# Squared key norms of the delta-rule branch from the diagonals of the key gram products

## Chip, cores and metric

The kernel runs on one core of one Trainium2 chip. The metric is the device time of one execution in microseconds, of which the median over several runs is given. Times inside an execution come from one profiled execution.

## What is computed

One layer of a diffusion backbone over 512 latent tokens with 256 context tokens, width 1024: modulated RMSNorm, one input projection that feeds two token mixers, their merge, then an expert-retrieval network and a final norm. The change lies in the first mixer, a bidirectional gated delta rule with 8 heads of 128 and chunks of 64 tokens. Of its reference this matters:

```python
def _l2norm(x):
    return x * lax.rsqrt(jnp.sum(x * x, axis=-1, keepdims=True) + EPS)
...
    k = _l2norm(_heads(k, A_HEADS))
...
    kb = k * beta[..., None]
    m = jnp.where(strict, jnp.einsum('bhnid,bhnjd->bhnij', kb, k) * decay, 0.0)
    a = m + jnp.eye(CHUNK, dtype=m.dtype)
...
    sol = lax.linalg.triangular_solve(a, rhs, left_side=True, lower=True, unit_diagonal=True)
```

So each head needs the norms of its 768 keys, and for each of its 12 chunks the 64x64 products of all keys with one another.

## The kernel before

The program has a prologue (norms, modulation, gates), the first branch (delta rule), the second branch (a gated linear scan), a tail of projections, the merge, and the expert network. The input projection is cut into 88 groups of 128 columns. Each group is done by `proj` as three matmuls per block of 128 rows (`mm3`, lines 103 to 105: the weights are split into a high and a low part), into the tiles `pcl` (512 latent columns) and `pcx` (256 context columns). The groups that the second branch and the merge need are called fills: `spill` projects them and sends them to DRAM, and they may be done at any time.

The first branch works head by head. `prepare(h)` makes what does not depend on the running state: the decays `E_`, the key norms, the chunk products `gl_`, the factors `br` (lines 572 to 574) and `brS` (576, 578) out of norms and gates, the inverse of each chunk's triangular matrix, then query, value and gate. `scan(h)` runs the 12 steps of the state recurrence in both directions. A step is a matmul of state and keys (L728, from its second step on), a DVE operation that makes `tmp` (L733), a matmul with the inverse (L735), a DVE operation that makes `vd` (L738), two matmuls for the new state (L744) and two DVE operations on the state (L752 copies into `sc_`, or L754).

Keys lie with their 128 channels on the partitions, tokens along the free axis (`kt`). Before, `norms(kt, 6)` squared them on ScalarE (L530) and summed over the partitions with matmuls against a column of ones (L532, one per block of 128 tokens, into the PSUM tile `pn`); `rsqrt` adds the epsilon on DVE (L195) and takes the power on GpSimd (L199). Then `gl_` is made by 12 matmuls of a chunk's keys with themselves (L570), each into one half of the partitions. The decays are multiplied by `br` on GpSimd (L582) and by `gl_` on DVE (L583). Of the product the 16x16 diagonal blocks are masked (`C_`, L587), summed into `D16` (L589) and sent through DRAM into `prob` (L595), where they are inverted (L599 to L616). The same function `norms` serves the queries.

The generators are interleaved: `weave` advances `scan(h)`, `prepare(h + 1)`, the rows of the modulation (`bacc`, `bw`) and the fills in fixed proportions, a piece from one `yield` to the next. On what they emit a scheduler then sets the order on each engine, with buffers and dependencies; each engine runs its own order strictly, but for weight loads. Also in the DVE order stand the low parts of the weights (`wlo`, L99), one per projection group.

Of the kernel before, what the change touches and what calls it, by code (L numbers as in the profile page):

```python
# [9 lines left out]
F32 = mybir.dt.float32  # L10
# [6 lines left out]
OP = mybir.AluOpType  # L17
AX = mybir.AxisListType.X
# [45 lines left out]
def program(nc, tc, A, out, dbg=None):  # L64
    V, S, G, T, Y = nc.vector, nc.scalar, nc.gpsimd, nc.tensor, nc.sync
# [18 lines left out]
    def bm(ap, n):  # L84

        return ap[:, None, :].to_broadcast([ap.shape[0], n, ap.shape[1]])
# [25 lines left out]
    def hct(shape, name, dt=F32):  # L112
        return hp.tile(shape, dt, name=name)
# [7 lines left out]
    ones1 = cst([128, 1], "ones1")  # L121
    m_st = [hct([128, 64], f"m_st{d}") for d in range(2)]
    m_in = [hct([128, 64], f"m_in{d}") for d in range(2)]
    m_in2 = hct([128, 2, 64], "m_in2")
    lvl2 = [hct([128, 2, 64], f"lvl2_{s}") for s in range(2)]
    dm4 = hct([128, 4, 16], "dm4")
# [13 lines left out]
    j64 = tmp_.tile([128, 64], I32, name="j64")  # L140
# [6 lines left out]
        G.iota(pl[s], pattern=[[0, 64]], base=0, channel_multiplier=1)  # L147
    V.tensor_scalar(m_st[0], j64, 0.0, None, op0=OP.is_lt)
    V.tensor_scalar(m_st[1], j64, 0.0, None, op0=OP.is_gt)
    V.tensor_scalar(m_in[0], j64, 0.0, None, op0=OP.is_ge)  # L150
    V.tensor_scalar(m_in[1], j64, 0.0, None, op0=OP.is_le)
    xr = tmp_.tile([128, 64], I32, name="xr")
# [41 lines left out]
    def rsqrt(dst, src, scale=1.0, eps=EPS):  # L194
        V.tensor_scalar(dst, src, scale, eps, op0=OP.mult, op1=OP.add)  # L195
        n = 1
        for x in dst.shape[1:]:
            n *= x
        G.tensor_tensor(dst, dst, mhalf[:dst.shape[0], :n], op=OP.pow)  # L199
# [15 lines left out]
    def bank(shape, name):  # L215
        return ps.tile(shape, F32, name=name, tag="a", bufs=3)
# [41 lines left out]
    with tc.tile_pool(name="p0", bufs=1) as p0:  # L258
# [41 lines left out]
        for k in range(KD):  # L300
            for z, bs in ((0, (0, 1, 2, 3)), (1, (4, 5))):
                pt = bank([128, NL], "pt")
                n = 128 * len(bs)
                for i, b in enumerate(bs):
# [6 lines left out]
                                                       op=OP.subtract)  # L311
# [96 lines left out]
    def blk(c, ctx):  # L408
        return (4 if ctx else 0) + c // 2, slice(64 * (c % 2), 64 * (c % 2) + 64), c % 2
# [63 lines left out]
    with tc.tile_pool(name="pA", bufs=1) as pA:  # L473
# [17 lines left out]
        def col(b):  # L491
            return b * 128 + (1 if b >= 4 else 0)

        def head(t, h):

            return t.rearrange("p b (d h) -> p d b h", d=2)[:, :, :, h]
# [30 lines left out]
        def norms(src, n):  # L527
            pn = bank([128, 8], "pn")
            sq = pA.tile([128, WG], F32, name="sq", tag="cv", bufs=CVB)
            S.activation(sq[:, :src.shape[1]], src, AF.Square)  # L530
            for b in range(n):
                T.matmul(pn[:, b:b + 1], sq[:, col(b):col(b) + 128], ones1, start=True, stop=True)  # L532
            r = pA.tile([128, n], F32, name=f"rn{n}", bufs=2)
            rsqrt(r, pn[:, :n])
            return r

        def ksl(kt, c, ctx):
            o = (NL + 1 if ctx else 0) + 64 * c
            return kt[:, o:o + 64]
# [9 lines left out]
        def prepare(h):  # L549
            if h == 0:  # L550
                yield from keys(0)
            kt = KT[h]
# [8 lines left out]
            S.activation(E_, E_, AF.Abs)  # L561
            S.activation(E_, E_, AF.Exp, scale=-1.0)
            yield
            rnk = bm(norms(kt, 6), 2)
            yield

            gl_ = bank([128, 6, 64], "gl_")
            for c in range(12):
                b, s, _ = blk(c % 8, c >= 8)
                T.matmul(gl_[s, b], ksl(kt, c % 8, c >= 8), ksl(kt, c % 8, c >= 8), start=True, stop=True)  # L570
            br = pA.tile([128, 3, 2, 6], F32, name="br", bufs=2)
            V.tensor_tensor(br[:, 0], head(beta, h), rnk, op=OP.mult)
            V.scalar_tensor_tensor(br[:, 1], br[:, 0], -1.0, rnk, op0=OP.mult, op1=OP.mult)
# [202 lines left out]
        rows_ = ada_rows()  # L776
        fill = chain(*fill)
        weave((prepare(0), 44), (fill, F0, True))
        for h in range(NH):
            weave((scan(h), WS), (prepare(h + 1) if h + 1 < NH else iter(()), 44), (rows_, 9, True),  # L780
                  (fill, FH if h < NH - 1 else FL, True))
# [678 lines left out]
```

## Time and profile before

| | |
|---|---|
| median of 3 runs | 2686.17 us (2684.44 to 2699.28) |
| profiled execution | 2690.35 us |
| its span | 2688.5 us |
| TensorE (PE) busy | 2499.1 us, 93% |
| TensorE weight loads (PEld) | 2097.6 us, 78% |
| VectorE (DVE) | 1867.9 us, 69% |
| ScalarE (ACT) | 1101.5 us, 41% |
| GpSimd (POOL) | 1142.4 us, 42% |

Busy time is the time in which an engine executes instructions of the kind named; PE and PEld overlap. An fp32 matmul shows as two rows. The idle time in brackets behind a row of a timeline is that of its engine just before it, with the instruction that ended it. The chain of waits is followed back from an engine's last instruction to what released it. The clock in the windows is TensorE's granted clock as a share of 2.4 GHz; its other level is 1.2 GHz.

### The profile page before, as it was taken

To read this page: it belongs to the slowest core of one execution; us is meant where nothing else is said; L and a number is where in the kernel's file an instruction comes from. 1 tells how busy PE (TensorE), PEld (TensorE's weight loads), DVE (VectorE), ACT (ScalarE), POOL (GpSimd) and SP (SyncE) were. 2 spreads that over 40 slices of the span, in tenths; PEclk is the share of its full clock that TensorE was granted. 3 is DMA by queue.
4 is the path that set the end of the run, shared out by engine and by line. 5 is a ranking of instruction groups with operands and counts; after the bars stand their busy time and mean duration, and the time that the engine had idled before them with its cause. 6 is when DMAs were issued, how large, how long until landed. Compare 5 with 4: busy or idle time off the path is not lost.

```text
span 2688.5 us, 40933 instructions
## 1 busy us (share of the span) xinstructions
PE 2499.1 (93%) x15664; PEld 2097.6 (78%) x15664; DVE 1867.9 (69%) x3260; ACT 1101.5 (41%) x1657; POOL 1142.4 (42%) x670
## 2 busy tenths in 40 slices
PE   6999999999999888999999878999999999999997
PEld 3777777777777767777778878898899989988886
DVE  6654565464464478834569998796887778778888
ACT  3533343343442466624322345455433333333333
POOL 2322233133240244300010555564577767777784
PEclk9999999899999989999999988999999999999999
DMA  5322233333241323336442477797898888899994
GB/s 213 102 80 77 79 105 95 84 94 99 82 115 60 122 96 106 110 114 200 161 144 90 144 247 269 265 321 249 291 362 315 314 307 312 308 327 331 328 327 157
DMA packets 247829, 511.08 MB, mean 190 GB/s; under 512 B 58784, under 2 KB 129856, under 8 KB 243536
## 3 DMA queue, kind: packets, MB, share of 16 engines
q1 hardware_dynamic: 190032, 318.64, 36.6%
q0 software_dynamic: 36864, 134.23, 13.9%
q10 hardware_dynamic: 20736, 55.58, 5.5%
q8 instruction: 123, 2.02, 0.3%
q14 instruction: 74, 0.61, 0.1%
HBM read 441.94 MB, written 66.44 MB: 189 GB/s over the span
## 4 chain that ended last, share of the span: by engine, by line
PE 63%; DVE 19%; DMA 5%; issue 5%; POOL 5%; ACT 3%; SPq 1%; DVEq 0%; POOLq 0%; ACTq 0%
PE oacc L104 6%; PE oacc L105 6%; PE oacc L103 6%; PE pcl L103 4%; PE pcl L105 4%; PE pcl L104 4%; PE pS L105 4%; PE pS L103 4%; PE pS L104 4%; DVE oh L1264 2%; DVE oh L1260 2%; DVE gscr L1126 2%; PE quad L744 2%; DVE wlo L99 1%; PE pq L105 1%
## 5 line engine op out<-in xcount | busy, mean ns | idle before, releaser
L99 DVE TENSOR_TENSOR wlo<-wraw,whi 128x1024 fp32r<-128x1024 f32 x328 | 511.6, 1560 | 199.2 <-ACT whi L98 189.7
L98 ACT CAST whi<-wraw 128x1024 fp32r<-128x1024 f32 x384 | 402.4, 1049 | 563.2 <-PE pS L104 158.4
L103 PE MATMUL pS<-tTh,whi 128*128 128x384 f32 x1024 | 351.2, 343 | 16.1 <-ACT afx L1024 15.2
L105 PE MATMUL pS<-tTh,wlo 128*128 128x384 f32 x1024 | 350.2, 342 | 11.9 <-POOL wlo L99 8.0
L104 PE MATMUL pS<-tTl,whi 128*128 128x384 f32 x1024 | 348.5, 340 | 0.0
L103 PE MATMUL oacc<-whi,ah 128*128 128x512 f32 x768 | 299.5, 390 | 5.1 <-ACT ah L1331 5.1
L105 PE MATMUL oacc<-whi,al 128*128 128x512 f32 x768 | 300.4, 391 | 0.9 <-DVE al L1332 0.9
L104 PE MATMUL oacc<-wlo,ah 128*128 128x512 f32 x768 | 300.2, 391 | 0.0
L103 PE MATMUL pcl<-hTh,whi 128*128 128x512 f32 x704 | 298.8, 424 | 0.0
L1327 POOL TENSOR_TENSOR ag<-af,gread 128x384 f32<-128x384 f32 x128 | 229.7, 1795 | 142.4 <-DVE al L1332 124.7
L104 PE MATMUL pcl<-hTl,whi 128*128 128x512 f32 x704 | 288.4, 410 | 0.0
L105 PE MATMUL pcl<-hTh,wlo 128*128 128x512 f32 x704 | 288.0, 409 | 0.0
L1123 POOL DMA_INDIRECT gr<-in_u_rows,eidx x128 | 188.3, 1471 | 133.8 <-DVE gscr L1126 98.3
L1123 POOL DMA_INDIRECT gr<-in_v_rows,eidx x128 | 210.5, 1644 | 41.2 <-DVE gacc L1130 20.4
L99 POOL TENSOR_TENSOR wlo<-wraw,whi 128x1024 fp32r<-128x1024 f32 x56 | 145.7, 2605 | 178.7 <-PE psc L1160 98.3
L103 PEld LDWEIGHTS pS<-tTh,whi 128*128 128x128 f32 x1024 | 196.6, 192 | 19.0 <-ACT afx L1024 15.8
L105 PEld LDWEIGHTS pS<-tTh,wlo 128*128 128x128 f32 x1024 | 196.3, 192 | 14.3 <-POOL wlo L99 9.5
L104 PEld LDWEIGHTS pS<-tTl,whi 128*128 128x128 f32 x1024 | 196.4, 192 | 2.0
L1331 ACT CAST ah<-ag 128x384 fp32r<-128x384 f32 x128 | 65.7, 513 | 300.3 <-PE oacc L104 289.8
L103 PEld LDWEIGHTS oacc<-whi,ah 128*128 128x128 f32 x768 | 144.6, 188 | 34.2 <-ACT ah L1331 5.6
L105 PEld LDWEIGHTS oacc<-whi,al 128*128 128x128 f32 x768 | 144.4, 188 | 31.7 <-DVE al L1332 1.6
L1126 DVE SCALAR_TENSOR_TENSOR gscr<-gr,ttk 128x1024 bf16<-128x1024 f32 x128 | 168.3, 1315 | 1.0
(1199 smaller groups left out, 5115.1 us busy)
## 6 DMA issues: line engine op xcount, KB each, us to landing
wraw<-in_u_t SPq DMA_DIRECT2D x128, 512.0 KB
wraw<-in_v_rows SPq DMA_DIRECT2D x128, 512.0 KB
wraw<-in_w_c SPq DMA_DIRECT2D x88, 512.0 KB
GD<-gst ACTq DMA_DIRECT2D x24, 1024.0 KB
gread<-GD SPq DMA_DIRECT2D x128, 192.0 KB
bw<-in_w_ada SPq DMA_DIRECT2D x64, 256.0 KB
afD<-afx ACTq DMA_DIRECT2D x64, 192.0 KB
af<-afD SPq DMA_DIRECT2D x64, 192.0 KB
```

Source lines behind the costliest of these rows:

```text
L98: S.copy(hi, raw)
L99: (eng or V).tensor_tensor(lo, raw, hi.bitcast(F32), op=OP.subtract)
L103: T.matmul(o, Lh, Rh, start=first, stop=False)
L104: T.matmul(o, Lh, Rl, start=False, stop=False)
L105: T.matmul(o, Ll, Rh, start=False, stop=last)
L744: T.matmul(po_[d], ktm[s, b], vd[s], start=True, stop=True)
L1123: G.indirect_dma_start(out=r, out_offset=None, in_=A["u_rows" if i < NSEL else "v_rows"], in_offset=IndirectOffsetOnAxis(ap=eidx[:, n:n + ...
L1126: x = V.scalar_tensor_tensor(scr, r, 1.0, ttk, op0=OP.mult, op1=OP.mult, accum_out=gs[:, n:n + 1])
L1260: V.tensor_tensor(oh1, io2[:, None].to_broadcast([128, 8, 128, 2]), over(sel[:, (tg * GT + t8) // 8].rearrange("p z t -> p (z t)")), op=OP ...
L1264: held[0] = V.tensor_tensor(oh2[:, 4 * z:4 * z + 4], oh1[:, 4:8], over(ghl[:, z, ts]), op=OP.mult)
L1327: G.tensor_tensor(ag.rearrange("p (g t) -> p g t", t=GT), af.rearrange("p (g t) -> p g t", t=GT), gr[:, :, e % EG, :], op=OP.mult)
L1331: S.copy(ah, ag)
```

## The change

The norms of the keys are no longer computed by `norms`. A mask `d64`, one where token and partition agree within a chunk, is made once. After the products `gl_` DVE multiplies them with the mask (`gd`) and sums over the 64 columns (`rnk`), which leaves each key's squared norm on the partition of its token; `rsqrt` follows as before. With `norms` one of the two `yield`s around it goes. The queries' norms are as they were.

```diff
--- before.py
+++ after.py
@@ -121,6 +121,7 @@
     ones1 = cst([128, 1], "ones1")
     m_st = [hct([128, 64], f"m_st{d}") for d in range(2)]
     m_in = [hct([128, 64], f"m_in{d}") for d in range(2)]
+    d64 = hct([128, 64], "d64")
     m_in2 = hct([128, 2, 64], "m_in2")
     lvl2 = [hct([128, 2, 64], f"lvl2_{s}") for s in range(2)]
     dm4 = hct([128, 4, 16], "dm4")
@@ -147,6 +148,7 @@
         G.iota(pl[s], pattern=[[0, 64]], base=0, channel_multiplier=1)
     V.tensor_scalar(m_st[0], j64, 0.0, None, op0=OP.is_lt)
     V.tensor_scalar(m_st[1], j64, 0.0, None, op0=OP.is_gt)
+    V.tensor_scalar(d64, j64, 0.0, None, op0=OP.is_equal)
     V.tensor_scalar(m_in[0], j64, 0.0, None, op0=OP.is_ge)
     V.tensor_scalar(m_in[1], j64, 0.0, None, op0=OP.is_le)
     xr = tmp_.tile([128, 64], I32, name="xr")
@@ -561,13 +563,18 @@
             S.activation(E_, E_, AF.Abs)
             S.activation(E_, E_, AF.Exp, scale=-1.0)
             yield
-            rnk = bm(norms(kt, 6), 2)
-            yield
 
             gl_ = bank([128, 6, 64], "gl_")
             for c in range(12):
                 b, s, _ = blk(c % 8, c >= 8)
                 T.matmul(gl_[s, b], ksl(kt, c % 8, c >= 8), ksl(kt, c % 8, c >= 8), start=True, stop=True)
+
+            gd = pA.tile([128, 6, 64], F32, name="gd")
+            V.tensor_tensor(gd, gl_, bm(d64, 6), op=OP.mult)
+            rnk = pA.tile([128, 6], F32, name="rnk", bufs=2)
+            V.reduce_sum(rnk, gd, axis=AX)
+            rsqrt(rnk, rnk)
+            rnk = bm(rnk, 2)
             br = pA.tile([128, 3, 2, 6], F32, name="br", bufs=2)
             V.tensor_tensor(br[:, 0], head(beta, h), rnk, op=OP.mult)
             V.scalar_tensor_tensor(br[:, 1], br[:, 0], -1.0, rnk, op0=OP.mult, op1=OP.mult)
```

The order on the engines moves with it. Here are three places; line numbers of the changed kernel are 7 higher than before from `br` on (L572 is L579, L583 is L590, L735 is L742, L738 is L745, L744 is L751, L752 is L759) and 2 higher for the rsqrt.

DVE at the start of `prepare(2)`, beside the first steps of `scan(1)`, before:

```order
L195 TENSOR_SCALAR rn_2259<-pn 128x6
L572 TENSOR_TENSOR br<-beta,rn_2259 128x12
L574 SCALAR_TENSOR_TENSOR br<-eg,rn_2259 128x12
L573 SCALAR_TENSOR_TENSOR br<-br,rn_2259 128x12
...
L99 TENSOR_TENSOR wlo<-wraw,whi 128x1024
L583 TENSOR_TENSOR E__2244<-E__2244,gl__2268 128x768
L738 TENSOR_SCALAR vd<-quad,edS 128x128
L589 TENSOR_REDUCE D_2295<-C__2293 128x192
L752 COPY sc__2317<-quad 128x128
```

and now:

```order
L573 TENSOR_TENSOR gd<-gl__2234,d_77 128x384
L575 TENSOR_REDUCE rnk<-gd 128x6
L197 TENSOR_SCALAR rnk<-rnk 128x6
L579 TENSOR_TENSOR br<-beta,rnk 128x12
L581 SCALAR_TENSOR_TENSOR br<-eg,rnk 128x12
L745 TENSOR_SCALAR vd<-quad,edS 128x128
L580 SCALAR_TENSOR_TENSOR br<-br,rnk 128x12
...
L99 TENSOR_TENSOR wlo<-wraw,whi 128x1024
L590 TENSOR_TENSOR E__2228<-E__2228,gl__2234 128x768
L759 COPY sc__2333<-quad 128x128
L759 COPY sc__2335<-quad 128x128
L596 TENSOR_REDUCE D_2267<-C__2265 128x192
```

The scan's `vd` has moved from behind the product of `E_` to the middle of `br`, and its copies `sc_` from behind `D16` to ahead of it.

PE at the same place, without the projections in between, before:

```order
L532 MATMUL pn<-ones_72,sq 128x1 x6
...
L570 MATMUL gl__2268<-kt 64x64 x12
L735 MATMUL quad<-vtm,TB 128x128
...
L744 MATMUL quad<-vd,ktm 128x128 x2
...
L728 MATMUL quad<-sc__2317,kt 64x128
```

and now:

```order
L570 MATMUL gl__2234<-kt 64x64 x12
...
L742 MATMUL quad<-vtm,TB 128x128
...
L751 MATMUL quad<-vd,ktm 128x128 x2
...
L735 MATMUL quad<-sc__2333,kt 64x128
```

The products stand where the norms stood. Of projections there were 6 between norms and products, none from there to the first matmul of the scan, then 6 and 18 (6 of these in the context's columns); now there are 6, 3 and 27.

DVE at the start of `prepare(6)`, beside `scan(5)`, before:

```order
L195 TENSOR_SCALAR rn_5870<-pn 128x6
L572 TENSOR_TENSOR br<-beta,rn_5870 128x12
...
L99 TENSOR_TENSOR wlo<-wraw,whi 128x1024
L583 TENSOR_TENSOR E__5855<-E__5855,gl__5879 128x768
L738 TENSOR_SCALAR vd<-quad,edS 128x128
```

and now:

```order
L573 TENSOR_TENSOR gd<-gl__5814,d_77 128x384
L745 TENSOR_SCALAR vd<-quad,edS 128x128
L575 TENSOR_REDUCE rnk<-gd 128x6
L759 COPY sc__5920<-quad 128x128
L197 TENSOR_SCALAR rnk<-rnk 128x6
L759 COPY sc__5922<-quad 128x128
L579 TENSOR_TENSOR br<-beta,rnk 128x12
...
L590 TENSOR_TENSOR E__5808<-E__5808,gl__5814 128x768
```

Here `vd` and both `sc_` stand ahead of `br`, and the `wlo` between `br` and the product of `E_` is gone.

## Rows read from the trace of the kernel before

**Rows 1.** The page: span, TensorE's busy time, the chain that ended last by engine.
```profile
span 2688.5 us, 40933 instructions
...
PE 2499.1 (93%) x15664; PEld 2097.6 (78%) x15664; DVE 1867.9 (69%) x3260; ACT 1101.5 (41%) x1657; POOL 1142.4 (42%) x670
...
PE 63%; DVE 19%; DMA 5%; issue 5%; POOL 5%; ACT 3%; SPq 1%; DVEq 0%; POOLq 0%; ACTq 0%
```

**Rows 2.** Windows (columns: start and end, length, busy us of each engine, clock, DMA).
```profile
95.00:895.00 800.00, 754.20 (x6209) 591.25 (x6208) 428.74 (x904) 312.31 (x548) 222.57 (x138) 0.97 0.31 90
```

**Rows 3.** Windows of seven openings: the second, the third and the sum.
```profile
258.60:282.40 23.80, 17.68 (x113) 13.59 (x111) 14.57 (x38) 6.87 (x10) 16.75 (x11) 0.91 0.53 157
...
361.90:385.00 23.10, 19.02 (x106) 13.74 (x105) 14.77 (x24) 7.24 (x11) 11.49 (x8) 0.85 0.49 140
...
sum 149.40, PE 121.15 PEld 91.28 DVE 92.89 ACT 41.02 POOL 72.22; mean PE 17.31 PEld 13.04 DVE 13.27 ACT 5.86 POOL 10.32
```

**Rows 4.** Windows of the seven stretches between the openings: their sum.
```profile
sum 527.70, PE 518.50 PEld 408.77 DVE 275.82 ACT 223.41 POOL 124.61; mean PE 74.07 PEld 58.40 DVE 39.40 ACT 31.92 POOL 17.80
```

**Rows 5.** Timeline of head 2's opening (start, duration, engine; in brackets the idle time).
```profile
258.60 1.39 PE L532 MATMUL pn<-ones,sq 128*128 128x1 f32 x12
...
258.71 1.21 DVE L99 TENSOR_TENSOR wlo<-wraw,whi 128x1024 fp32r<-128x1024 f32 x1
...
260.27 1.34 POOL L199 TENSOR_TENSOR rn<-rn,mhalf 128x6 f32<-128x6 f32 x1 [3.22 <-DVE rn L195]
...
261.42 0.92 PE L570 MATMUL gl__2268<-kt 128*64 128x64 f32 x24
...
262.16 1.48 POOL L582 TENSOR_TENSOR E__2244<-E__2244,br 128x768 f32<-128x768 f32 x1 [0.56 <-DVE br L573]
...
263.70 2.25 DVE L99 TENSOR_TENSOR wlo<-wraw,whi 128x1024 fp32r<-128x1024 f32 x1
...
265.88 0.94 DVE L583 TENSOR_TENSOR E__2244<-E__2244,gl__2268 128x768 f32<-128x768 f32 x1
...
266.74 0.34 DVE L738 TENSOR_SCALAR vd<-quad,edS 128x128 f32<-128x128 f32 x1
...
267.13 0.49 PE L744 MATMUL quad<-vd,ktm 64*128 64x128 f32 x4 [2.98 <-DVE vd L738]
...
282.40 0.79 PE L735 MATMUL quad<-tmp,TB 128*128 128x128 f32 x2 [3.13 <-DVE tmp L733]
```

**Rows 6.** Chain of waits, 255 to 284 us (start, duration, piece).
```profile
254.87 0.23 PE pcl L104
...
274.56 3.15 DMA praw<-dd
...
282.08 0.27 DVE tmp L733
...
283.19 0.43 PE pcl L104
```

**Rows 7.** Tile sq: the two kinds of row that go (ns, least/median/most).
```profile
L532 PE MATMUL pn<-ones,sq x160: 165/250/371, 102.0 to 779.7; 128*128 128x1 f32 x160
...
L530 ACT ACTIVATE sq<-kt x8: 830/847/851, 101.1 to 742.1; 128x769 f32<-128x769 f32 x8
```

**Rows 8.** Lines 694 and 611: the nearest rows for the added operations.
```profile
L694 DVE TENSOR_TENSOR T<-T,z x32: 541/554/555, 150.8 to 830.5; 128x384 f32<-128x384 f32 x32
...
L611 DVE TENSOR_REDUCE w__787<-t__786 x1: 286/286/286, 129.0 to 129.0; 112x32 f32<-112x128 f32 x1
...
L611 DVE TENSOR_REDUCE w__796<-t__795 x1: 686/686/686, 131.2 to 131.2; 112x64 f32<-112x512 f32 x1
```

**Rows 9.** Chain of waits, 250 to 370 us: the query's norm and gram products.
```profile
290.33 0.79 PE pn L532 x8
...
291.11 0.62 PE gq__2459 L630 x16
```

**Rows 10.** Waits of TensorE, 195 to 775 us (sum, times, longest).
```profile
PE quad L744 <- DVE vd L738: 15.2, 10, 3.3
```

## Prediction

> **What bounds the kernel now.** I read the page first. The span is 2688.5 us, the profiled execution took 2690.35 us, and the median of the runs is 2686.17 us, 0.16% less; I make the sum against the execution and put the difference on the median. PE is busy for 93% of the span and carries 63% of the chain that ended last [rows 1]. Every engine's order is the same in both programs from the end of the second branch on, so only the first 1160 us can change. The operations that change lie in the first branch, 95 to 895 us; in the second the same rows are shifted against one another. In the first branch PE is busy 754.20 of 800 us [rows 2].
>
> Next I cut that stretch where PE stands still. Each head h from 1 to 7 has an *opening*. It runs from the first matmul of the key norms (`pn`) in `prepare(h)` to the matmul of `scan(h-1)` that waits behind the copy to `prob`. The seven openings last 149.40 us in all, and PE is busy for 121.15 of it; the granted clock is down to 0.85 in the third [rows 3]. In the seven stretches between them PE is busy 518.50 of 527.70 us [rows 4]: these are full, and what leaves them shortens the kernel. In the openings there are 28 us of idle PE, and somewhat more for the time at 1.2 GHz.
>
> Head 2 shows what sets an opening's length [rows 5]. The twelve `pn` rows (each fp32 matmul leaves two) take 1.39 us, the rsqrt's power on POOL 1.34, then `br`, the product of E_ on POOL (1.48) and on DVE (0.94). The chain of waits goes on through POOL, then over the round trip of the diagonal blocks to DRAM (3.15 us for its last leg), `prob`, and the scan's `tmp` [rows 6]. That is a chain of latencies, started by the norms. PE fills it with projection matmuls and runs dry twice in head 2: 2.98 us for `vd`, which stands on DVE behind the product of E_, and 3.13 us for `tmp`, behind `prob` [rows 5, 6]. After the second stop the projections start 0.43 us apart, not 0.23: the clock's lower level [rows 6].
>
> **The change part by part.** *Removed.* Per head twelve `pn` rows, 1.39 us of PE, 8 x 1.39 = 11.1 us, and one Square on ACT of 0.85 us [rows 7]; ACT is busy for 312 of the 800 us [rows 2], and a Square that starts later or not at all is waited for by nobody but `pn`, so I cost it at nothing. What it would cost if ACT filled up: the same 0.85 us as a gain.
>
> *Added.* The mask product `gd` reads 384 elements out of PSUM. The row of the same size and source is L694's 554 ns: 0.55 us. The reduction of 384 elements lies between the rows of 128 and of 512 inputs, 286 and 686 ns; on the line between them 0.55 us [rows 8]. Bounds: 0.29 and 0.69. The constant d64 is one small operation before the stretch, under work that waits for loads: nothing. Both operations stand on the chain, and DVE, busy for 429 of 800 us [rows 2], has room for the 8 x 1.1 us.
>
> *The chain.* Before: `pn`, 1.39. Now: `gl_` (0.92 [rows 5]) + 0.55 + 0.55 = 2.02. The power and all behind it is as before. That is +0.63 per opening, 7 x 0.63 = +4.4. The DVE order adds and takes. One `vd` (0.34 [rows 5]) stands between the reduction and E_'s product in h = 1, 2 and 4: +1.0 in all. A `wlo` (1.21 alone [rows 5]) and a `vd` stand there in h = 3 and 7: +3.1. A `wlo` in h = 5: +1.2. In h = 6 the reduction waits for `vd` and the rsqrt for a copy `sc_`, so behind nine projections (9 x 0.23) and two small matmuls of the scan: about 2.0 in place of none. Sum +7.3. Against it, the `wlo` that stood between `brS` and E_'s product goes in h = 3 and 6: between 1.21 (alone) and 2.25 us (beside POOL [rows 5]) each; 1.7 taken, -3.4. Chain: 4.4 + 7.3 - 3.4 = **+8.3 us**.
>
> *What PE does meanwhile.* The yield that goes lets `gl_` come where `pn` was, and lets the scheduler fill the opening with other rows. Counted in both orders from `pn` (now `gl_`) to the matmul behind `prob`, over h = 1 to 7: 292 of `pcl` and 78 of `pcx` before, 379 and 66 now. At 0.23 and half of that [rows 6], 87 x 0.23 - 12 x 0.12 = 18.6 us of projections move out of full stretches into openings. In h = 3 the query's norm and its gram products (0.79 + 0.62 us [rows 9]) move too: 1.4. Total **-20.0 us**. `vd` now stands ahead of E_'s product in all seven heads, so PE's waits for it (15.2 us in ten of them, three of these elsewhere [rows 10]) shrink; PE then meets the second stop earlier, which is why I count moved work against the chain's length and not the waits themselves. Behind `vd` now: the rest of `br`, 0.35 us, already in the chain. If `gl_`'s PSUM buffer is held longer (until E_'s product, as before, but from an earlier start), the next to want one is `pbg` or `gq_`, many microseconds on: nothing.
>
> *Head 0* has no scan beside it: 1.39 off PE, 0.63 on the chain, -0.8.
>
> Sum: 8.3 - 20.0 - 0.8 = **-12.5 us**: 2690.35 becomes 2678 in a profiled execution, and the median 2686.17 becomes **2674 us**. A measurement of this kernel can tell about 0.5%, or 13.4 us, from no change, so this is just inside.
>
> The weight loads are busy 591.25 of 800 us in this stretch, 74%, against 94% for the matmuls [rows 2]. The Trainium skill, Perfetto Trace Analysis, section Identifying the Most-Contended Engine, says that matmul busy time is a poor measure of TensorE's headroom and that the busy share of the weight loads is to be taken: by that a quarter of PE would be free, the 20.0 us would bring nothing, and the sum would be the chain's +8.3. The row speaks for the matmuls: outside the stops they start 0.23 us apart without a break [rows 6], and 518.50 of 527.70 us are filled.
>
> **The rivals.** *1. The stops go and do not come back.* For it: `vd` leads in every head; of the waits for it some 12 us are in openings [rows 10], and the clock takes 2.1 + 3.5 us more in h = 2 and 3 (what the mean clock lacks to 1.00, 0.09 and 0.15, times 23.80 and 23.10 us [rows 3]). Against: `prob` still waits for the same round trip. 11.1 + 12 + 5.6 = 28.7 less: **2658 us** (2657.5). Chance 0.22.
>
> *2. Only PE's own work goes.* Chain and filler cancel, and the eight groups of `pn` are what is left: -11.1, **2675 us**. Chance 0.2.
>
> *3. The chain decides (slower).* The product of E_ comes later by 8.3 us over the seven openings, and the projections moved into them are missed later: the scan's steps then wait for their own DVE operations where projections covered them. It decides once PE's share in the stretches between openings falls by the 20.0 us moved, from 98.3% to under 95% [rows 4]. 2686.17 + 8.3: **2694 us**; with `gd` and the reduction at 0.69 each and the h = 6 wait twice as long, 2699 or a little more. For it: openings are set by latency today. Against: the stretches between are full by a margin. Chance 0.14.
>
> **How the numbers follow.** My forecast has 0.42; its own range is 2666 to 2681 (the reduction's bounds, 0.3 x 8; the `wlo` that goes, 1.0 x 2; a third of the moved rows). 0.02 is for what I have not named. Beyond -13.4 us lie 0.19 of the forecast, 0.22 of rival 1 and 0.02 of rival 2: faster 0.43. Slower by more than 0.5% is 0.05 of rival 3 and the 0.02: 0.07. Within: 0.50. The range must hold rival 1's 2658 and most of rival 3, **2658 to 2691 us**; it leaves out half of rival 1 below and some of rival 3 above.
>
> **What would show it.** 64 matmul rows of `pn` left of 160 [rows 7], `gd` near 0.55 and the reduction near 0.55 us. PE's busy time in the first branch down by some 11 us. Waits of L744's matmuls (now L751) for `vd` in openings at most about 1 us; the stop behind `prob` still there, not longer than before by more than 2 us. If the openings are shorter than now, rival 1 is right and the chain was over-costed; if PE's share between openings falls under 95%, rival 3. If `gd` or the reduction takes over 1 us, the term of the chain is wrong.

## Result, and the profile after

The changed kernel takes 2712.43 us (median; 2706.71 to 2719.38), the kernel before on the same chip 2686.2. The ratio is 1.0085, with a 95% interval of 1.0068 to 1.0102: 23 us slower, where 12.5 us faster was forecast. The profiled execution took 2719.38 us. All comparisons below are such ratios, each with the kernel before run beside it; 0.1% is 2.7 us. Two executions far above the rest (3420.70 us of the kernel before, 6017.73 of b_hold) are left out of the ratios. The others of a kernel lie some 10 us to either side of their median, at most 18, so traces are used for where time lies, not for how much a version gains.

The page of the kernel after, against [rows 1]:

```profile
span 2717.6 us, 40736 instructions
...
PE 2512.6 (92%) x15568; PEld 2106.1 (77%) x15568; DVE 1872.2 (69%) x3277; ACT 1095.0 (40%) x1649; POOL 1131.7 (42%) x670
```

Windows of the kernel after (start and end, length, busy us of each engine, clock, DMA): the first branch, against [rows 2], then the second and the third opening, against [rows 3].

```profile
95.00:895.00 800.00, 733.13 (x5938) 572.59 (x5936) 419.78 (x900) 298.74 (x526) 218.53 (x138) 0.95 0.30 87
...
262.18:287.62 25.44, 18.96 (x112) 14.16 (x111) 15.69 (x27) 8.03 (x12) 16.02 (x12) 0.97 0.53 167
369.96:398.94 28.98, 26.10 (x155) 19.19 (x155) 20.69 (x57) 9.37 (x12) 11.35 (x7) 0.94 0.38 118
```

In the same 800 us PE is busy 21 us less than in [rows 2], and its mean clock is 0.95 in place of 0.97 (what it lacks to 1.00 goes from 24 to 40 us). The openings hold more PE work, as forecast, the third 26.10 us in place of 19.02; but they are longer by nearly as much, and the stretches between did not shorten in return. Here are the seven openings and the six stretches between them, each as a sum, in the kernel before (an opening ends here with the first product of `tmp` issued behind `prob`):

```profile
sum 156.00, PE 127.75 PEld 96.24 DVE 97.97 ACT 44.96 POOL 73.24; mean PE 18.25 PEld 13.75 DVE 14.00 ACT 6.42 POOL 10.46
...
sum 455.52, PE 447.23 PEld 354.11 DVE 235.07 ACT 195.03 POOL 106.60; mean PE 74.54 PEld 59.02 DVE 39.18 ACT 32.50 POOL 17.77
```

and in the kernel after:

```profile
sum 183.45, PE 157.93 PEld 117.95 DVE 116.64 ACT 51.82 POOL 72.60; mean PE 22.56 PEld 16.85 DVE 16.66 ACT 7.40 POOL 10.37
...
sum 449.95, PE 420.03 PEld 332.65 DVE 215.52 ACT 183.81 POOL 103.69; mean PE 70.00 PEld 55.44 DVE 35.92 ACT 30.64 POOL 17.28
```

The openings took in 30.2 us of PE work and grew by 27.5; PE stands idle in them for 25.5 us, before for 28.3. (In three of the seven the matmul that ends the opening now belongs to the scan's fourth step in place of the third, so a part of what moved is the border itself.) 27 us of PE work have left the stretches, and they are 5.6 us shorter. PE's share there fell from 98.2% to 93.4%. Over both together, where the border plays no part, PE is idle for 18.9 us more and busy for 3.0 us more. What it waits for is in TensorE's waits, 95 to 895 us (sum, times, longest), before:

```profile
PE quad L744 <- DVE vd L738: 15.7, 11, 3.3
PE quad L735 <- DVE tmp L733: 11.9, 7, 3.1
...
PE quad L1394 <- DVE on L1391: 2.6, 3, 1.1
```

and after:

```profile
PE quad L1401 <- DVE on L1398: 22.8, 6, 7.7
PE quad L742 <- DVE tmp L740: 21.8, 12, 4.4
PE quad L751 <- DVE vd L745: 6.3, 5, 2.7
```

The waits for `vd` shrank by 9.4 us, and those for `tmp` grew by 9.9. The wait for `on` is new in this size. L1401 (L1394 before) are the transposes in `finish`, the last thing that each scan does: squares of the head's output on ScalarE, their scaling by the query's norm (`ssq`, twice, then the rsqrt with its power on GpSimd, then `s_fin`), the product `on`, and PE's transposes of it. None of the prediction's steps went there. PE at the end of `scan(0)`, from the last product of the scan's output to the transposes, before and after:

```profile
246.61 1.96 PE L770 MATMUL quad<-vn,qk 64*64 64x128 f32 x32
...
253.15 0.60 PE L1394 MATMUL quad<-ident,on 128*128 128x128 f32 x4
```

```profile
249.18 1.96 PE L777 MATMUL quad<-vn,qk 64*64 64x128 f32 x32
...
259.26 0.63 PE L1401 MATMUL quad<-ident,on 128*128 128x128 f32 x4 [2.35 <-DVE cols L464]
```

That is 4.6 us before and 8.1 after. Summed over the first six heads it is 30.0 and 54.7 us, in the last two as before. DVE in the finish of `scan(0)`, timeline, before:

```profile
249.79 0.23 DVE L1383 TENSOR_TENSOR ssq<-ssq,s_fin 128x4 f32<-128x4 f32 x1 [6.73 <-ACT scr_f L1380]
250.06 0.16 DVE L1384 TENSOR_TENSOR ssq<-ssq,s_fin 128x4 f32<-128x4 f32 x1
250.25 0.17 DVE L195 TENSOR_SCALAR ssq<-ssq 128x4 f32<-128x4 f32 x1
251.61 0.16 DVE L1386 TENSOR_TENSOR s_fin<-s_fin,ssq 128x4 f32<-128x4 f32 x1 [1.19 <-POOL ssq L199]
251.88 0.69 DVE L1391 TENSOR_TENSOR on<-quad,s_fin 128x512 f32<-128x512 f32 x1
252.48 0.55 DVE L694 TENSOR_TENSOR T<-T,z 128x384 f32<-128x384 f32 x1
253.07 2.83 DVE L698 TENSOR_TENSOR TB<-T,br 64x768 f32<-64x768 f32 x1
```

and after:

```profile
251.89 0.55 DVE L701 TENSOR_TENSOR T<-T,z 128x384 f32<-128x384 f32 x1 [8.62 <-PE z L693]
252.37 0.23 DVE L1390 TENSOR_TENSOR ssq<-ssq,s_fin 128x4 f32<-128x4 f32 x1
252.51 0.94 DVE L705 TENSOR_TENSOR TB<-T,br 64x768 f32<-64x768 f32 x1
253.47 1.03 DVE L708 TENSOR_TENSOR TB<-T,br 64x512 f32<-64x512 f32 x2
254.53 0.17 DVE L1391 TENSOR_TENSOR ssq<-ssq,s_fin 128x4 f32<-128x4 f32 x1
254.73 0.17 DVE L197 TENSOR_SCALAR ssq<-ssq 128x4 f32<-128x4 f32 x1
256.08 2.30 DVE L1393 TENSOR_TENSOR s_fin<-s_fin,ssq 128x4 f32<-128x4 f32 x1 [1.18 <-POOL ssq L201]
258.42 0.69 DVE L1398 TENSOR_TENSOR on<-quad,s_fin 128x512 f32<-128x512 f32 x1
```

T and TB, the end of `prepare(1)`, have moved from behind `on` to ahead of the rsqrt, here and in the five heads that follow. That is 2.0 us for the three products of TB. The power on GpSimd then ends later, and the next operation in GpSimd's order, the product `qd` of `scan(1)`, meets `s_fin`. GpSimd's timeline at that place, before and after:

```profile
250.57 1.01 POOL L199 TENSOR_TENSOR ssq<-ssq,mhalf 128x4 f32<-128x4 f32 x1 [0.56 <-DVE ssq L195]
252.71 2.38 POOL L710 TENSOR_TENSOR qd<-qd,qn 128x1024 f32<-128x1024 f32 x1 [1.13 <-ACT qd L709]
```

```profile
255.04 1.01 POOL L201 TENSOR_TENSOR ssq<-ssq,mhalf 128x4 f32<-128x4 f32 x1 [2.47 <-DVE ssq L197]
256.02 2.35 POOL L717 TENSOR_TENSOR qd<-qd,qn 128x1024 f32<-128x1024 f32 x1
```

Before, `qd` waited for ScalarE and began 1 us after `s_fin`. After, both begin together and end together: `s_fin` takes 2.30 us for 128x4 elements in place of 0.16. Tile `s_fin` (least, median, most ns), before and after:

```profile
L1386 DVE TENSOR_TENSOR s_fin<-s_fin,ssq x7: 161/162/164, 251.6 to 840.4; 128x4 f32<-128x4 f32 x7
```

```profile
L1393 DVE TENSOR_TENSOR s_fin<-s_fin,ssq x7: 164/2300/2309, 256.1 to 864.2; 128x4 f32<-128x4 f32 x7
```

Why T and TB moved is in `weave`. It hands out turns by `(turn + 1) / share`, the share of `prepare` being 44 per head, that of the scan 14. The change takes one yield, so every piece of `prepare` behind it comes one turn earlier against the scan, the last of them, T and TB, included. **Theory Y:** the piece that went is the loss, by T and TB ahead of the finish. **Rival N:** the norms out of the diagonals are themselves the loss.

### The profile page after: what moved, and what is told of

Same layout as the page of the kernel before. It is cut to its first block, busy times and chain, and to the rows that moved or that the text cites. A ratio compares the mean times of both kernels' runs of the same rounds, so it can differ in the third digit from the quotient of the medians.

```text
span 2717.6 us, 40736 instructions
## 1 busy us (share of the span) xinstructions
PE 2512.6 (92%) x15568; PEld 2106.1 (77%) x15568; DVE 1872.2 (69%) x3277; ACT 1095.0 (40%) x1649; POOL 1131.7 (42%) x670
## 4 chain that ended last, share of the span: by engine, by line
PE 39%; DVE 11%; issue 2%; DMA 2%; ACT 1%; POOL 1%; SPq 0%; DVEq 0%; POOLq 0%; ACTq 0%
PE oacc L105 6%; PE oacc L104 6%; PE oacc L103 6%; PE pS L105 4%; PE pS L103 4%; PE pS L104 4%; DVE oh L1271 2%; DVE oh L1267 2%; DVE gscr L1133 2%; PE pq L105 1%; PE pq L103 1%; PE pq L104 1%; DVE eq L1231 1%; PE pcl L105 1%; PE pcl L103 1%
## 5 line engine op out<-in xcount | busy, mean ns | idle before, releaser
L104 PE MATMUL pcl<-hTl,whi 128*128 128x512 f32 x704 | 294.6, 418 | 0.0
L104 PEld LDWEIGHTS oacc<-wlo,ah 128*128 128x128 f32 x768 | 144.4, 188 | 29.3
```

Source lines behind the costliest of these rows:

```text
L104: T.matmul(o, Lh, Rl, start=False, stop=False)
```

## The experiments

Each ratio rests on 5 to 12 executions of the kernel. For the traces one more measure is used: the start of the scan's product with TB (L735 before, L742 after) in each of the 12 steps of 8 scans, compared with the kernel before. What this lag changes from the last step of a scan to the first of the next is summed as "handovers" (seven; the finish lies there), the rest as "inside scans". The last column is the lag at the last step; it also holds the lag at the first.

| kernel | ratio to before (95%) | handovers | inside scans | last step |
|---|---|---|---|---|
| changed kernel | 1.0085 (1.0068 to 1.0102) | +14.5 | +11.3 | +25.3 |
| b_noyield | 1.0083 (1.0056 to 1.0110) | +26.4 | +4.5 | +30.8 |
| a_yield | 0.9947 (0.9927 to 0.9967) | -8.3 | -5.4 | -15.5 |
| a_yield_late | 0.9974 (0.9958 to 0.9990) | -7.3 | +1.2 | -9.5 |
| a_yield_prob | 0.9972 (0.9960 to 0.9984) | -3.1 | +1.2 | -2.0 |
| a_sfinpool | 1.0019 (1.0003 to 1.0036) | -3.9 | +15.2 | +10.6 |
| b_sfinpool | 0.9973 (0.9958 to 0.9989) | +0.2 | -3.2 | -5.6 |
| a_yield_sfin | 0.9947 (0.9928 to 0.9966) | -8.3 | -6.5 | -18.8 |
| a_yield_pn | 0.9967 (0.9951 to 0.9983) | 0.0 | -12.9 | -13.6 |
| a_yield_chain | 0.9944 (0.9929 to 0.9958) | -8.4 | -12.7 | -20.7 |
| a_yield_chain4 | 1.0040 (1.0025 to 1.0055) | -8.2 | +15.3 | +8.5 |
| a_tbhold3 | 1.0037 (1.0022 to 1.0053) | +2.6 | +2.4 | +4.6 |
| b_yield3 | 1.0021 (1.0002 to 1.0041) | +10.0 | +5.7 | +14.5 |
| a_w43 | 0.9984 (0.9970 to 0.9999) | -7.6 | +12.1 | +1.3 |
| a_yield_hold | 0.9898 (0.9882 to 0.9915) | -4.8 | -7.3 | -16.4 |
| b_hold | 0.9969 (0.9953 to 0.9984) | +2.6 | -0.4 | -0.8 |

**The yield without the norms (b_noyield).** The kernel before, its own norms kept:

```diff
             rnk = bm(norms(kt, 6), 2)
-            yield
```

> The kernel before, with only the yield behind the norms taken out; the norms stay as they were. Theory Y (the yield that went lets three products of prepare's next level, TB, into DVE's order ahead of the rsqrt of the scan's finish, and PE's transposes wait there): +20 to +30 us, 2706 to 2718, and PE's waits for `on` in 95 to 895 us of about 20 us in place of 2.6. Rival N (the norms out of the diagonals themselves are the cost: a later product of E_, and the added DVE operations): no change, 2680 to 2692.

1.0083, as slow as the whole change. Waits of its TensorE in the first branch:

```profile
PE quad L1393 <- DVE on L1390: 21.4, 6, 6.2
PE quad L743 <- DVE vd L737: 18.6, 11, 3.2
PE quad L734 <- DVE tmp L732: 5.8, 7, 3.4
```

The wait for `on` is there (21.4 us), with the old norms and the old waits for `vd`, and time and wait are both as theory Y had them. Rival N falls.

**A piece put back, at three places.** The changed kernel with one yield more: ahead of `gl_` (a_yield), behind the rsqrt (a_yield_late), behind the copy to `prob` (a_yield_prob).

```diff
+            yield
             gl_ = bank([128, 6, 64], "gl_")
```

> The changed kernel with a second yield put back where the norms stood, ahead of the products gl_. In DVE's order the finish is again ahead of TB in every head. Theory Y: 10 to 15 us below before at best and 2 below at least, 2671 to 2684; waits for `on` about 3 us again. Rival N: as the changed kernel, 2706 to 2718.

> The changed kernel with a second yield put in behind the rsqrt, ahead of br. The finish stands ahead of TB here too. Theory Y: 2671 to 2686, as with the yield ahead of gl_, since only the number of pieces matters for the finish. Rival P (it matters where the opening is cut, since filler goes to the pieces): the two yields differ by more than 8 us. Rival N: 2706 to 2718.

> The changed kernel with a second yield far behind the norms, after the copy to prob: gl_, the mask product and the reduction come in the same piece as in the changed kernel, but prepare has as many pieces again as before. Theory Y (the number of pieces decides where TB stands against the scan's finish): 2671 to 2686, waits for `on` about 3 us in the first branch. If the loss came from the piece with the norms itself: 2706 to 2718.

All three are faster than before, by 14, 7 and 7.5 us, and 30 to 37 us faster than the changed kernel. TensorE's waits of a_yield:

```profile
PE quad L743 <- DVE tmp L741: 22.4, 9, 5.6
PE quad L752 <- DVE vd L746: 5.7, 3, 4.3
...
PE quad L1402 <- DVE on L1399: 3.3, 4, 1.1
```

`on` is back to 3.3 us (3.5 in a_yield_late; 5.3 in a_yield_prob, where about 3 were expected: in one head `s_fin` meets `qd` there too, for 2.30 us, without T or TB ahead of it). The seven openings and the six stretches of a_yield:

```profile
sum 187.97, PE 160.23 PEld 118.93 DVE 121.23 ACT 58.42 POOL 74.90; mean PE 22.89 PEld 16.99 DVE 17.32 ACT 8.35 POOL 10.70
...
sum 411.66, PE 405.06 PEld 319.65 DVE 214.25 ACT 178.87 POOL 103.64; mean PE 67.51 PEld 53.27 DVE 35.71 ACT 29.81 POOL 17.27
```

The stretches are 44 us shorter than before and 98.4% full. But the openings are 32.0 us longer, with 32.5 us more of PE work and as much idle time as before (27.7 us against 28.3); five of them end a scan step later. Over both together a_yield has 9.7 us less of busy PE, as much as seven `pn` of 1.39 us, and 2.2 us less of idle PE. So what moved into the openings filled next to nothing there. Between a_yield and a_yield_late lie 7 us by the ratios, whose intervals overlap a little, and 9.7 by the medians, on either side of the 8 that were to tell rival P: whether the place counts is not settled.

**The small product off DVE (a_sfinpool, b_sfinpool, a_yield_sfin).** In `finish`, in the changed kernel, in the one before and in a_yield:

```diff
-        V.tensor_mul(s, s, ssq)
+        G.tensor_tensor(s, s, ssq, op=OP.mult)
```

> The changed kernel, with the finish's small product s*ssq (128x4) of the first branch on GpSimd instead of DVE, so that it stands ahead of the qd product there and doesn't run beside it; TB stays ahead of the rsqrt on DVE. If the 2.30 us that s_fin takes beside qd are about half of what is lost per head (2 us in each of six heads): 2698 to 2706. If the three TB products ahead of it are the whole loss: 2708 to 2718.

> The kernel before, with the finish's small product s*ssq of the first branch on GpSimd instead of DVE. There it did not run beside the qd product (0.16 us), so if its move in the changed kernel paid by ending that meeting: no change here, 2682 to 2694. If the move pays for another reason (DVE relieved): as much below before as the changed kernel with it is below the changed kernel, 10 to 18 us.

On GpSimd `s_fin` takes 0.20 us ahead of `qd`:

```profile
255.82 0.20 POOL L1393 TENSOR_TENSOR s_fin<-s_fin,ssq 128x4 f32<-128x4 f32 x1
255.97 2.38 POOL L717 TENSOR_TENSOR qd<-qd,qn 128x1024 f32<-128x1024 f32 x1
```

The waits for `on` fall from 22.8 to 13.4 us, and the time by 18 us (1.0085 to 1.0019), more than the 6 to 14 expected. The control gains 7 us by its ratio, beyond its interval, though its median of 2682.88 still lies in the range for no change; its handovers are unchanged (+0.2), so those 7 have another source, which the runs don't show. If the same 7 are in both, the meeting is worth some 11. On top of a_yield the move gives nothing:

> The kernel with a yield put back ahead of gl_, and the finish's small product on GpSimd. If the 0.3% that this move gave the kernel before holds here too: 2665 to 2670, the fastest. If it was in the order of that kernel alone: 2670 to 2680, as the yield alone.

0.9947, as the yield alone; no meeting was left there to end. So the meeting is worth 11 to 18 of the 37 us. Against a_yield_sfin, which has the same move, a_sfinpool still lacks 19 us: with T and TB ahead of the finish but no meeting, its handovers are 4.4 us behind (-3.9 and -8.3), the inside of its scans 21.7, and the way from the scan's last product to the transposes is 42.4 us in the first six heads, between the 30.0 and 54.7 above.

**T and TB held behind the finish (a_tbhold3, a_yield_hold, b_hold).** The last products of `levels` (z1, T, TB) wait for the finish to be emitted, in the changed kernel, in a_yield and in the kernel before:

```diff
+                    while s_ == 1 and d == 1 and scanned[0] < h:
+                        yield
                     z1 = bank([128, 6, 64], "z1")
...
-            while scanned[0] < h:
-                yield
...
-            scanned[0] += 1
...
             finish(nc, pA, quad, rsqrt, po, rnq, 128 ** -0.5, ident, small["gnw"], ga, oaD[h], False, bc)
+            scanned[0] += 1
```

> The changed kernel with its one yield, in which the last products of the levels (z1, T and TB) are held until the scan's finish is emitted; on DVE the finish then stands ahead of T and TB in heads 0 to 5, with no piece added. Theory Y: waits for `on` of about 3 us again and 2676 to 2692 (TB itself comes later, which the next scan's first step may miss). If the loss comes from something else that the missing piece moves: 2704 or more, though the waits for `on` go.

> The kernel with a yield put back ahead of gl_, and in it T and TB held until the finish is emitted. If holding them has a price of its own (less cover for PE behind the last po matmul, TB later for the next scan): 8 to 18 us above the kernel with the yield alone, 2680 to 2692. If holding costs nothing: 2668 to 2678, and what is left of the loss with T and TB held is the piece count's elsewhere.

> The kernel before, with its own norms and pieces, and T and TB held until the scan's finish is emitted. If the two gains add up (0.5% for the norms, 0.5% for the hold): 0.995 of before, 2671 to 2680. If the hold pays only together with the new norms: no change, 2682 to 2692. If all of the 1.0% is the hold: 2658 to 2668, and the norms out of the diagonals give nothing beside it.

a_tbhold3 lies between the two theories at 1.0037. Its waits:

```profile
PE quad L742 <- DVE tmp L740: 23.2, 11, 3.8
PE quad L1400 <- DVE on L1397: 10.7, 7, 4.2
```

Half of the wait for `on` is left: z1 no longer fills PE while the finish computes, and in the first six heads 13 to 15 rows of projections are all that stands between the scan's last product and the transposes. (In a_yield_hold, without z1 there too, they are 18 in five of the six, and the wait is 4.2 us.) No `s_fin` meets `qd`, and the way to the transposes is 28.5 us in these heads, no longer than before. The hold gives 13 us here. But it gives 13 also in a_yield, where no TB stood ahead of the finish, and 8 in the kernel before. So it does not isolate that order: theory Y is right about the piece, but T and TB ahead of the finish are not shown to be all of the loss, and the missing piece costs 37 us with the hold (0.9898 to 1.0037) as without (0.9947 to 1.0085). a_yield_hold, 27 us under before, is faster than either of its expectations and the fastest version found, faster than both kernels. b_hold lies between its first two (0.995 and no change): of the 1.0%, 0.3% are the hold's, and 0.7% come with the norms (0.9898 / 0.9969). By which wait the hold pays in a_yield, the traces don't show.

**Turns in place of pieces (a_w43, b_yield3).** The changed kernel with other shares, and the kernel before with a third yield:

```diff
-            weave((scan(h), WS), (prepare(h + 1) if h + 1 < NH else iter(()), 44), (rows_, 9, True),
+            weave((scan(h), WS), (prepare(h + 1) if h + 1 < NH else iter(()), 43), (rows_, 9, True),
```

> The changed kernel, its one yield as it is, with prepare's share in weave at 43 in place of 44 turns per head, which spreads the pieces as far as they reached before. On DVE the finish stands ahead of T and TB again. If the number of pieces against the turns is the cause: 2671 to 2686, as with a yield put back. If the missing yield costs in another way: 2695 or more.

> The kernel before with one more yield behind the norms, three where two were. If a piece more is what makes the kernels with a yield put back faster than before, and not the norms out of the diagonals: 2671 to 2680. If the number of pieces that before has is what fits: 2684 to 2700.

At 43 turns, with no piece added, 27 of the 37 us are back (1.0085 to 0.9984), and the median of 2685.57 is at the upper end of the first range. The handovers are as in a_yield (-7.6), the inside of the scans is not (+12.1). In b_yield3 a piece more makes the kernel before no faster, rather 6 us slower, as its second range had it. So a_yield does not gain by more pieces as such: of the counts tried in the kernel before, two yields, which is what 44 turns go with, are the best.

**What the norms cost (a_yield_pn, a_yield_chain, a_yield_chain4).** a_yield with the old Square and `pn` done again for nobody, and with the mask product and the reduction repeated once, or four times:

```diff
             V.reduce_sum(rnk, gd, axis=AX)
+            V.tensor_tensor(gd, gd, bm(d64, 6), op=OP.mult)
+            V.reduce_sum(rnk, gd, axis=AX)
```

> The kernel with a yield put back ahead of gl_, and the removed Square on ScalarE and six fp32 matmuls per head (pn) done again behind gl_; nobody reads their result. If the gain of the diagonal norms is PE's own work (8 x 1.39 us): 10 to 12 us above the kernel with the yield alone (2675 there), 2685 to 2688. If the gain comes from projections that fill the openings: the twelve rows fall into an opening where PE has stops, and it stays within 4 us, 2673 to 2680.

> The kernel with a yield put back ahead of gl_, with the mask product and the reduction each done twice in a row (same result), so that the chain from gl_ to prob is about 1.0 us longer per head. If openings are set by that chain: 7 openings x 1.0 = 7 us above the kernel with the yield alone, 2680 to 2684, plus up to 4 for the clock. If projections cover it: 2673 to 2678.

> The kernel with a yield put back ahead of gl_, with four more pairs of mask product and reduction in a row: 4 x 1.09 = 4.4 us more on the chain from gl_ to prob in every head. If projections cover the chain up to there too: within 5 of the kernel with the yield alone, 2670 to 2680. If it is on the path from some point on: up to 7 x 4.4 = 31 us above, 2690 to 2706.

`pn` done again costs 5 us by the ratios, with intervals that overlap; its median of 2677.09 is in the second range, not in the first. In the trace the six handovers from `scan(0)` on go from -1.4 each to 0.0, the price of `pn` [rows 5], and the inside of the scans is 7.5 us shorter, which one execution of each can't tell from chance. Once 1.1 us more on the chain costs nothing (0.9944). 4.4 us more per head cost 25 us of the 31 on the chain. The chain has a slack that ends between these, unless it is DVE, 4.4 us busier in every head, that costs here: the runs don't separate the two.

## Why the prediction was wrong

**The step that failed** is the one on what PE does meanwhile: "what leaves them shortens the kernel", 20.0 us. It took the time of the rows that move into openings as gained, and counted the two orders in the openings alone. Neither held.

- In the openings the moved rows did not fill idle time. The scan's next product stands behind them in PE's order, and the openings grew by nearly what came in: 27.5 us for 30.2 in the changed kernel, 32.0 for 32.5 in a_yield. Over openings and stretches PE's idle time fell by 2.2 us in a_yield, not by 20.
- Outside them the yield moved every later piece of `prepare` by a turn against the scan, and in the stretches "full by a margin" the finish, a chain over ScalarE, DVE, GpSimd and DVE, lost its place on DVE in six of eight heads. From the scan's last product to the transposes these six take 24.7 us more (54.7 for 30.0; 30.0 again in a_yield).

In the order with a piece less the new norms give nothing (1.0083 without them, 1.0085 with). Shown: the yield alone makes the kernel before as slow (b_noyield), and a piece put back anywhere, or 43 turns, takes most or all of it away. Of the distance between the traces of the changed kernel and a_yield, 23 us stand in the handovers (from -8.3 to +14.5), where the finish lies, and 17 inside the scans. Of the finish, the meeting of `s_fin` and `qd` is shown to cost (a_sfinpool). How much the rest is, T and TB ahead of it, is not: in a_tbhold3 the finish has its place back, and the missing piece costs 37 us all the same. The part inside the scans stays open as well: the waits for `tmp` are as long in a_yield (22.4 us) as in the changed kernel (21.8).

**The sum without that step.** With the pieces as many as before, the same norms give -14 us (a_yield) or -7.5 (a_yield_prob, whose norms are computed in the piece where the change has them), against the forecast's -12.5. That it comes close is luck, since its two large terms, of opposite sign, were both not paid.

- *Removed*: 1.4 us in each of six handovers, the price of `pn`. The rule of the Trainium skill that the prediction weighed (Perfetto Trace Analysis, section Identifying the Most-Contended Engine) judges TensorE's headroom by the weight loads' busy share, 74% here, beside the share of peak work; as the prediction read it, the 20.0 us would bring nothing. They brought next to nothing, but the runs don't tie that to room between the weight loads. Nor does `pn` done again test the rule, since each of its rows has a weight load of its own (160 of either in the kernel before, the loads 192 ns each).
- *Added*: right. Tile `gd` in the kernel after:

```profile
L575 DVE TENSOR_REDUCE rnk<-gd x8: 543/550/553, 101.6 to 778.7; 128x6 f32<-128x384 f32 x8
L573 DVE TENSOR_TENSOR gd<-gl__717,d x1: 558/558/558, 101.0 to 101.0; 128x384 f32<-128x384 f32 x1
```

- *The chain*, +8.3: the length was near, the price was not. From the first `gl_` (`pn`) to the end of the copy to `prob` the seven openings take 138.2 us against 134.1, +4.1, and in a_yield 146.5, +12.4, in a kernel that is faster; and a chain longer by 1.1 us per head did not lengthen the kernel at all.
- *The stop behind `prob`* was to grow by at most 2 us: the longest wait for `tmp` went from 3.1 to 4.4, within that, but there are 12 in place of 7, 21.8 us in place of 11.9. The waits for `vd` stayed above the forecast's 1 us in one opening (2.7).

**The rivals.** Rival 3 had the sign, and its sign in the profile came true (PE's share between openings under 95%). Rival 1 wanted shorter openings; they grew. Rival 3's mechanism, a later product of E_, is not what the runs show, and its price of 8 us was a third of the loss. Rival N of the experiments, its successor, fell with the first run. Rival 2, that chain and filler cancel and PE's own work goes, is near a_yield's time, and what a_yield's trace lacks of busy PE is as much as seven `pn`; but a_yield_pn gives back only 5 of its 11 us, so it stays unproven. The chance of 0.07 for slower was too small because no term had been given to places outside the openings.

## What to carry over

Where a yield goes in a kernel whose parts are interleaved by shares, the order must be read again at every place where the two parts meet, above all behind the last matmul of a part, where PE depends on a short chain over other engines. Change the shares with the number of pieces, or keep the pieces. Work that moves into a gap is gained only as far as idle time falls: sum busy and idle time over a stretch whose ends don't move. To learn whether the new arithmetic or the new order costs, take the yield out of the old kernel: one run told it here.

## What the runs showed of the hardware

A DVE operation of 128x4 elements took 2.30 us, fourteen times its 0.16, when it began 0.06 us after a GpSimd product of 2.35 us, and it ended 0.01 us behind it. TB's first product shows the same: 2.83 us where it began during `qd` (before), 0.94 where it did not (after). In a_yield_hold one `s_fin` took 1.25 us, beside a GpSimd product of 1.29. GpSimd's product took 2.35 to 2.38 us in either case. The Trainium skill, SBUF — State Buffer, section SBUF: two separate sides, says that a DVE operation with two SBUF inputs and a GpSimd operation that reads SBUF take an exclusive lock for a whole instruction, and that the one that comes second is blocked. The rows agree: the price of such a meeting is about what is left of the other engine's operation (2.14 us for 2.29 left, 1.89 for 2.02), however small one's own is. The prediction had the same effect in a row, a `wlo` of 1.21 us that took 2.25 beside GpSimd [rows 5], there a `bacc` that began at 263.60 us, and used it only inside the openings.
